# Attention in two levels of Strassen products: the sums of K's second chunk ten slots later, and the first batch's V sums later in the opening

## The chip, the cores and the metric

The kernel runs on one core of one Trainium2 chip. The metric is the time of one execution on the device, in microseconds, as the median of several runs. A core has a matrix engine (TensorE, PE in the profile), a vector engine (VectorE, DVE), a scalar engine (ScalarE, ACT), GpSimd (POOL) and SyncE (SP). Each runs its own list of instructions in the order in which the program wrote them; semaphores tie the lists together. Here SyncE issues the stores of the output and the DMA transposes, and GpSimd issues the loads.

## What is computed

For 8 batches, q, k and v are 2048 x 512 (float32, normal random numbers):

```python
scores = np.matmul(q, k.transpose(0, 2, 1)) / np.sqrt(d_k)
attn_weights = special.softmax(scores, axis=-1).astype(np.float32)
return np.matmul(attn_weights, v)
```

## The kernel before

**Products.** All matrices are cast to float16, and sums of products are float32 in PSUM. Both matrix products are done in a form of Strassen's method: a product of 2 x 2 blocks is made with seven block products instead of eight, and pays for it with sums of blocks ahead of them and sums of results behind them. For Q K^T the operands' sums are four per chunk of K (`k_sums`, lines 181 to 190; the four are L185, L186, L187 and L188, in that order, and L186 overwrites a block of K in place) and four per 1024 queries of Q (`q_sums`, L202 to L205). For P V they are four per half of V (`v_sums`, L219 to L222) and four per tile of P (`p_sums`, L368 to L371). Some P V products are split a second time (`fine`, lines 500 to 550; its sums are `a_sums`, L494 to L497, and `vi_sums`, L241 to L244). The operands' sums are all on VectorE.

**Results.** `Group` (line 285) makes the scores of 256 keys by 1024 queries with its seven products (L317). Product 5 starts a PSUM bank z, product 3 adds to it, and VectorE's L342 (`after3`) adds z to a tile `cz` and so empties the bank; L339 (`after7`) does the same for the bank x after product 7. ScalarE copies and takes the exponential (L253; the one over `cz` is the largest). `Pair` (line 378) multiplies P by V (L414), and its results are scaled by the reciprocal of the row sums, which a column of ones in V gives (L423 on ScalarE, L426 on VectorE). In `fine`, ScalarE's L530 and L534 copy partial results out of PSUM, and VectorE's L536 and L541 add them.

**Order.** The order is written out by hand. The work goes in 32 periods, four per batch (`qt` = 0 to 3), each of 28 slots. A slot holds one product of a Group, for the scores of the next 1024 queries, and often one product of a Pair for the output of the present period. Beside each slot stand the sums that VectorE is to do there (`sums_of`, line 615) and the loads, transposes and K sums for the next batch (`prefetch`, line 601). A slot thus sets a place in each engine's list and not a time.

**The next batch's K.** K comes in four chunks of 512 keys. For each, GpSimd loads it with a cast into a staging tile (two of these exist), SyncE transposes it by DMA into the tile `kraw` of that chunk (L150), and VectorE then does the four sums. `PLAN` (line 577) gives the slots of loads and transposes; for the second chunk the transpose stands at slot 8 of period 1 and for the third at slot 20 of period 1. `KSUMS` (line 592) gives the slots of the sums, counted through the batch's four periods: 39 is slot 11 of period 1, 56 is slot 0 of period 2. All this is done in the first seven batches, for the batch that follows. The first Group of the next batch that uses the second chunk begins at slot 14 of period 2; its product with the first sum stands at slot 16, with the third at slot 17, and with the fourth at slot 19.

**The opening.** Ahead of the periods stand 14 slots with the first scores of the first batch, in which VectorE takes one sum per slot from a list called `background` (line 599; `step`, line 758). In the first period `SUMS0` (line 661) names VectorE's sums: "v11" is the sum number 1 of the half 1 of V. The half 0 of V is loaded by two transfers and the half 1 by the two last ones of the opening.

Of the kernel before, what the change touches and what calls it, by code (L numbers as in the profile page):

```python
# [12 lines left out]
def kernel(  # L13
# [153 lines left out]
    def pe_transpose(what, c, n0=0, n1=CH):  # L167
        for n in range(n0, n1, 2):
            transposed(what, c, n, 2, nc.scalar.copy if n and n0 != n else nc.vector.tensor_copy)
# [28 lines left out]
    def q_sums(sp):  # L198
        b11, b12, b21, b22 = q_blocks(sp)
        t1, t2, t4 = qsum  # L200
        return [
            lambda: sub(t1[:], b12, b11),  # L202
            lambda: sub(t2[:], b22, t1[:]),
            lambda: sub(t3_of(sp), b22, b12),
            lambda: sub(t4[:], b21, t2[:]),  # L205
        ]
# [6 lines left out]
    def v_sums(b, c):  # L213
        vh = vraw[b % 2]
        js = slice(c * NI, (c + 1) * NI)
        b11, b12 = vh[:, js, 0, 0:H], vh[:, js, 0, H:D]
        b21, b22 = vh[:, js, 1, 0:H], vh[:, js, 1, H:D]
        return [
            lambda: sub(vt1[:, js, 0:H], b12, b11),  # L219
            lambda: sub(vt2[:, js], b22, vt1[:, js, 0:H]),  # L220
            lambda: sub(b12, b22, b12),
            lambda: sub(vt4[:, js], b21, vt2[:, js]),  # L222
        ]
# [31 lines left out]
    def plain_tile(kb, half, name):  # L255

        st = bank(name)
        c, n = divmod(kb, CH)
        for dc in range(ND):
            nc.tensor.matmul(  # L260
                st[:], kops[c][0][:, n, dc, :], qraw[0][:, half * NT:(half + 1) * NT, dc, :],
                start=(dc == 0), stop=(dc == ND - 1),
            )
        left, right = pts[0]
        exp(right[:, kb // 2, kb % 2, :] if half else left[kb % 2][:, kb // 2, :], st[:])
# [89 lines left out]
    def p_sums(g, which, j0=0, j1=NJ):  # L355

        left, right = pts[g // 2]
        if (g, which) not in psums:
            psums[g, which] = [
                spool.tile([P, NJ, P], F16, tag=f"s{n}", name=f"s{n}") for n in (1, 2, 4)  # L360
            ]
        s1, s2, s4 = psums[g, which]
        cols = columns(g, which)
        js = slice(j0, j1)
        a11, a21 = left[0][:, js, cols], right[:, js, 0, cols]
        a12, a22 = left[1][:, js, cols], right[:, js, 1, cols]
        return [
            lambda: add(s1[:, js], a21, a22),  # L368
            lambda: sub(s2[:, js], s1[:, js], a11),  # L369
            lambda: sub(a21, a11, a21),  # L370
            lambda: sub(s4[:, js], a12, s2[:, js]),  # L371
        ]
# [205 lines left out]
    for qt_, slot_, *what_ in (  # L578
# [13 lines left out]
    KSUMS = {  # L592
        divmod(slot, NS): (c, n)
        for c, slots in (
            (0, (39, 42, 43, 44)), (1, (46, 48, 56, 59)), (2, (67, 71, 74, 76)), (3, (84, 86, 88, 90))
        )
        for n, slot in enumerate(slots)
    }
    background = deque()
# [15 lines left out]
    def sums_of(g, slot):  # L615
# [43 lines left out]


    SUMS0 = {
# [96 lines left out]
    def step(n=1):  # L758
        for _ in range(min(n, len(background))):
            background.popleft()()  # L760
# [19 lines left out]
    for slot in range(14):  # L780
        n, at = divmod(slot, len(QORDER))
        old, what = QORDER[at]
        if slot == 3:
            background.extend(p_sums(0, "a", 0, NG))
            background.append(v_sums(0, 0)[0])
        if slot == 7:
            background.extend((v_sums(0, 1)[0], v_sums(0, 0)[1]))
        if at == 0:
            cur = Group(0, 6 + n)
        if old == 0:  # L790
            cur.product(what)
        elif prev is not None:
            prev.product(what)
        if at == 2 and prev is not None:
            prev.exp_right()
        if at == len(QORDER) - 1:
            prev = cur
        if slot in TILES:
            plain_tile(*tiles.pop(0), "px")
        if slot in (8, 10):  # L800
            pe_transpose("q", 3, slot - 8, slot - 6)
        if slot in (10, 12, 13):
            q_sums(1)[max(slot - 11, 0)]()
        step()
# [56 lines left out]
```

## Time and profile before

| | |
|---|---|
| median of 3 runs | 823.46 us (822.53 to 823.62) |
| the profiled execution | 824.57 us |
| its span, first to last instruction | 822.5 us |
| mean granted TensorE clock in it | 0.996 |
| VectorE busy | 677.8 us |
| ScalarE busy | 609.1 us |
| HBM traffic over the span | 163 GB/s |

The profile is one execution. A row of a table of instructions gives the source line, the engine, the operation, the tile written, an arrow and the tiles read, the shapes, how many there were, their busy time and what ended the idle time before them. A row of a timeline begins with the start and the length in microseconds, and ends, in brackets, with how long the engine had been idle before and which engine, tile and line released it. SPq and POOLq are issues of DMAs. TensorE's ends are modelled, so its busy time is not a measure of its efficiency; its idle time, which is what the waits show, is read from starts.

### The profile page before, as it was taken

What the parts mean: (1) busy time and instruction counts of PE and PEld (TensorE: products, weight loads), DVE (VectorE), ACT (ScalarE), POOL (GpSimd) and SP (SyncE); (2) the same over time, 40 slices, a digit from 0 to 9 for tenths busy, and PEclk for the clock granted to TensorE, in tenths of its full rate; (3) what the DMA queues carried; (4) which work ended last, traced back from release to release, by engine and by line L of the source; (5) the groups of instructions that cost most, each with busy time, mean ns of one, the idle gap of its engine ahead of it and who ended that gap; (6) DMA issues with size and microseconds to landing.
All of it is one profiled execution on the core that took longest, in us unless ns stands there. A gap on an engine that the chain in (4) does not pass through costs nothing.

```text
span 822.5 us, 16565 instructions
## 1 busy us (share of the span) xinstructions
PE 792.6 (96%) x6226; PEld 537.8 (65%) x6226; DVE 677.8 (82%) x1568; ACT 609.1 (74%) x1194; POOL 72.1 (9%) x106
## 2 busy tenths in 40 slices
PE   8999899998999899997999989999899998999998
PEld 5556566665666566665666656666566665666676
DVE  3788788969899698995889968898788987889774
ACT  4678677876877777776777877878687776787752
POOL 4011110101100110001100011001110101000000
PEclk9999999999999999999999999999999999999999
DMA  9989992899928999289983899657994679811112
GB/s 220 167 145 141 170 215 70 160 155 194 172 60 162 159 185 173 70 155 140 188 168 78 154 154 196 138 109 147 162 198 103 139 140 173 164 55 53 52 52 103
DMA packets 188160, 115.96 MB, mean 141 GB/s; under 512 B 122288, under 2 KB 170800, under 8 KB 188080
## 3 DMA queue, kind: packets, MB, share of 16 engines
q0 software_dynamic: 49648, 49.29, 41.0%
q1 hardware_dynamic: 138144, 65.29, 34.5%
q8 instruction: 48, 0.79, 0.4%
q10 hardware_dynamic: 288, 0.33, 0.1%
q14 instruction: 32, 0.26, 0.1%
HBM read 100.73 MB, written 33.55 MB: 163 GB/s over the span
## 4 chain that ended last, share of the span: by engine, by line
PE 79%; DMA 16%; DVE 3%; ACT 1%; issue 1%; POOL 0%; DVEq 0%; ACTq 0%
PE t L317 38%; PE t L414 31%; DMA kraw<-stage 12%; PE t L519 10%; DMA vh<-in_v_dram 3%; DMA right<-in_q_dram 1%; ACT right L253 1%; DVE cz L342 1%; DMA first<-in_k_dram 1%; DVE cz L339 0%; DVE o L426 0%; DVE s L369 0%; DVE left L496 0%; DVE kraw L186 0%; POOL stage L124 0%
## 5 line engine op out<-in xcount | busy, mean ns | idle before, releaser
L317 PE MATMUL t<-qraw,kraw 128*128 128x512 f16 x728 | 206.4, 379 | 0.2 <-ACT left L253 0.2
L414 PEld LDWEIGHTS <-s 128*128 128x128 f16 x1536 | 150.5, 98 | 60.0 <-issue 1.6
L253 ACT ACTIVATE left<-t 128x512 f16<-128x512 f32 (+1 forms) x260 | 155.7, 602 | 23.3 <-PE t L317 17.4
L423 ACT ACTIVATE o<-t,r 128x256 f32<-128x256 f32 x256 | 116.1, 483 | 56.1 <-DVE r L443 30.1
L317 PE MATMUL t<-qs,ks 128*128 128x512 f16 x488 | 136.1, 381 | 19.2 <-DVE cz L342 19.2
L253 ACT ACTIVATE right<-cz 128x1024 f16<-128x1024 f32 x122 | 129.3, 1060 | 17.0 <-DVE cz L339 16.3
L414 PE MATMUL t<-vt,s 128*128 128x257 f16 (+1 forms) x1024 | 135.6, 275 | 0.0
L414 PEld LDWEIGHTS <-right 128*128 128x128 f16 x1024 | 100.2, 98 | 37.2 <-issue 0.5
L333 ACT COPY cz<-t 128x512 f32<-128x512 f32 x120 | 70.3, 586 | 68.2 <-PE t L317 65.3
L317 PEld LDWEIGHTS <-kraw 128*128 128x128 f16 x976 | 90.5, 98 | 44.9 <-issue 1.0
L426 DVE SCALAR_TENSOR_TENSOR o<-t,r,o 128x256 f32<-128x256 f32 x192 | 92.2, 480 | 23.2 <-ACT o L530 8.9
L317 PEld LDWEIGHTS <-ks 128*128 128x128 f16 x732 | 66.6, 97 | 59.7 <-issue 21.3
L339 DVE TENSOR_TENSOR cz<-t,cz 128x512 f32<-128x512 f32 x122 | 83.7, 686 | 22.2 <-PE t L317 21.5
L519 PEld LDWEIGHTS <-left 128*128 128x128 f16 x928 | 69.2, 98 | 45.4 <-issue 5.2
L342 DVE TENSOR_TENSOR cz<-t,cz 128x512 f32<-128x512 f32 x122 | 83.8, 687 | 13.7 <-PE t L317 7.1
L328 ACT COPY t<-t 128x512 f32<-128x512 f32 x120 | 69.0, 575 | 20.0 <-PE t L317 15.9
L317 PE MATMUL t<-qs,kraw 128*128 128x512 f16 x244 | 73.2, 382 | 0.1
L317 PE MATMUL t<-qraw,ks 128*128 128x512 f16 x244 | 72.5, 378 | 0.0
L336 ACT COPY cz<-t 128x512 f32<-128x512 f32 x122 | 71.1, 583 | 0.0
L519 PE MATMUL t<-vh,left 128*128 128x128 f16 x696 | 67.6, 219 | 3.0 <-ACT o L530 3.0
L414 PE MATMUL t<-vh,s 128*128 128x257 f16 x512 | 66.9, 272 | 0.2 <-ACT o L423 0.2
L414 PE MATMUL t<-vt,right 128*128 128x256 f16 x512 | 66.2, 273 | 0.3 <-DVE o L426 0.3
(85 smaller groups left out, 937.2 us busy)
## 6 DMA issues: line engine op xcount, KB each, us to landing
out_dram<-o SPq DMA_DIRECT2D x127, 256.0 KB, 2.9
vh<-in_v_dram POOLq DMA_DIRECT2D x32, 512.0 KB, 10.2
stage<-in_q_dram POOLq DMA_DIRECT2D x28, 512.0 KB, 6.7
stage<-in_k_dram POOLq DMA_DIRECT2D x28, 512.0 KB, 6.4
right<-in_q_dram POOLq DMA_DIRECT2D x2, 512.0 KB, 9.9
right<-in_k_dram POOLq DMA_DIRECT2D x2, 512.0 KB, 12.1
first<-in_q_dram SPq DMA_DIRECT2D x2, 256.0 KB, 3.9
cz<-in_q_dram SPq DMA_DIRECT2D x2, 256.0 KB, 4.9
```

Of the source, the lines that this page charges most:

```text
L253: nc.scalar.activation(out=out_, in_=in_, func=EXP, scale=inv_sqrt_d)
L317: nc.tensor.matmul(dst[:], lhs[:, j, dc, :], rhs[:, :, dc, :], start=(n in (1, 5) and dc == 0), stop=(dc == 1), skip_group_check=True,)
L328: f(out=self.y[:], in_=self.x[:])
L333: f(out=self.cz[:, 1, :], in_=self.z[:])
L336: nc.scalar.copy(out=self.cz[:, 0, :], in_=self.x[:])
L339: nc.vector.tensor_add(self.cz[:, 1, :], self.x[:], self.cz[:, 1, :])
L342: nc.vector.tensor_add(self.cz[:, 0, :], self.z[:], self.cz[:, 0, :])
L414: nc.tensor.matmul(dst[:, 0:width], lhs(j), rhs(j), start=(first and j == 0), stop=(j == NJ - 1), skip_group_check=True,)
L423: nc.scalar.activation(out=out_, in_=src, func=COPY, scale=r[:])
L426: nc.vector.scalar_tensor_tensor(out=out_, in0=src, scalar=r[:], in1=out_, op0=MULT, op1=ADD)
L519: nc.tensor.matmul(dst, lhs[:, j, :], rhs[:, j, :], start=(n == 1 and j == 0), stop=(j == NI - 1), skip_group_check=True,)
```

## The change

```diff
@@ -592,7 +592,7 @@
     KSUMS = {
         divmod(slot, NS): (c, n)
         for c, slots in (
-            (0, (39, 42, 43, 44)), (1, (46, 48, 56, 59)), (2, (67, 71, 74, 76)), (3, (84, 86, 88, 90))
+            (0, (39, 42, 43, 44)), (1, (56, 59, 60, 65)), (2, (67, 71, 74, 76)), (3, (84, 86, 88, 90))
         )
         for n, slot in enumerate(slots)
     }
@@ -659,7 +659,7 @@
     SUMS0 = {
-        2: "v11", 4: "q3", 5: "a0", 6: "a1", 8: "a3", 9: "a2", 
+        2: "v01", 3: "v11", 4: "q3", 5: "a0", 6: "a1", 8: "a3", 9: "a2", 
         12: "v20", 14: "b0 v21", 15: "v30", 16: "b1",
@@ -782,9 +782,8 @@
         if slot == 3:
             background.extend(p_sums(0, "a", 0, NG))
-            background.append(v_sums(0, 0)[0])
         if slot == 7:
-            background.extend((v_sums(0, 1)[0], v_sums(0, 0)[1]))
+            background.extend(v_sums(0, 0)[0:2])
         if at == 0:
             cur = Group(0, 6 + n)
```

The four sums of the second chunk move from slots 18 and 20 of period 1 and 0 and 3 of period 2 to slots 0, 3, 4 and 9 of period 2. In VectorE's list the first sum now stands where the third stood, behind two instructions of period 1's last Pair; the second, third and fourth follow three to ten instructions apart.

In the opening, the first sum of V's half 0 keeps its place in VectorE's list, because four sums of P are ahead of it in `background` either way. The first sum of V's half 1, which came next, moves to slot 2 of the first period, and the second sum of the half 0 takes the place that it leaves. The second sum of the half 1 moves from slot 2 to slot 3, right behind.

The numbers of instructions on every engine are the same before and after, and the lists of TensorE, ScalarE, GpSimd and SyncE hold the same instructions in the same order.

## The prediction

> **What bounds the kernel now.** I read the page first, then the table of waits, then the timelines of the places that the waits name. The page's first part and its chain by engine:
>
> ```profile
> PE 792.6 (96%) x6226; PEld 537.8 (65%) x6226; DVE 677.8 (82%) x1568; ACT 609.1 (74%) x1194; POOL 72.1 (9%) x106
> ...
> PE 79%; DMA 16%; DVE 3%; ACT 1%; issue 1%; POOL 0%; DVEq 0%; ACTq 0%
> ```
>
> TensorE is busy 792.6 of 822.5 us, so about 30 us of it can be idle at most, and yet 16% of the chain is DMA. Something makes the end wait for transfers now and then. The table of waits, of TensorE and then of VectorE (total us, times, longest):
>
> ```profile
> PE t L317 <- DVE cz L342: 19.2, 7, 4.2
> PE t L519 <- ACT o L530: 3.0, 5, 0.6
> PE t L728 <- DVE warm L683: 1.2, 1, 1.2
> PE t L260 <- DVE qraw L163: 1.0, 1, 1.0
> ```
>
> ```profile
> DVE ks L185 <- DMA kraw<-stage: 31.5, 7, 6.0
> ```
>
> TensorE waits seven times, 19.2 us in all, for VectorE's add of line 342; VectorE waits seven times, 31.5 us, in the first sum of a K chunk (L185) for the DMA transpose that writes this chunk. Seven is the number of batches for which a next batch is prepared. The timelines of the second of the seven, VectorE, then TensorE, then ScalarE:
>
> ```profile
> 181.62 0.17 DVE L477 RECIPROCAL r<-t 128x1 f32<-128x1 f32 x1 [0.48 <-PE t L414]
> 185.70 0.42 DVE L185 TENSOR_TENSOR ks<-kraw 128x512 f16<-128x512 f16 x1 [3.90 <-DMA kraw<-stage]
> 186.04 0.68 DVE L342 TENSOR_TENSOR cz<-t,cz 128x512 f32<-128x512 f32 x1
> ...
> 188.17 0.68 DVE L339 TENSOR_TENSOR cz<-t,cz 128x512 f32<-128x512 f32 x1
> ...
> 193.68 0.41 DVE L187 TENSOR_TENSOR ks<-ks,kraw 128x512 f16<-128x512 f16 x1
> ```
>
> ```profile
> 186.78 0.59 PE L317 MATMUL t<-qs,ks 128*128 128x512 f16 x2 [2.14 <-DVE cz L342]
> ...
> 190.15 0.39 PE L519 MATMUL t<-vh,left 128*128 128x128 f16 x4 [0.59 <-ACT o L530]
> ```
>
> ```profile
> 188.88 1.06 ACT L253 ACTIVATE right<-cz 128x1024 f16<-128x1024 f32 x1 [0.89 <-DVE cz L339]
> 189.85 0.25 ACT L530 COPY o<-t 128x128 f32<-128x128 f32 x1
> ```
>
> This is one event from end to end. At 181.8 VectorE reaches the first sum of K's second chunk and stands 3.90 us. Behind it in VectorE's order stands L342, which empties the PSUM bank that the next fifth product needs: TensorE stands 2.14 us. L339 is late too, so ScalarE's exponential is late, L530 behind it is late, and TensorE stands 0.59 us more. Of VectorE's wait the first 3.90 - 2.14 = 1.76 us cost nothing. The row at 193.68, the third sum, marks slot 0 of the next period (39 of the sums' list is slot 11 of period 1, so 56 is slot 0 of period 2): there the change puts the first sum.
>
> **The change, part 1: K's second chunk.** Per batch four VectorE instructions of 0.42 us move from slots 18 and 20 of period 1 and slots 0 and 3 of period 2 to slots 0, 3, 4 and 9 of period 2. No instruction is added and no DMA moves. In the order written for VectorE, L342, L426, L339 and the rest of period 1 come ahead of the wait.
>
> The first batch's wait shows the same (TensorE):
>
> ```profile
> 87.57 0.59 PE L317 MATMUL t<-qs,ks 128*128 128x512 f16 x2 [3.07 <-DVE cz L342]
> ```
>
> Term a: the seven waits for L342, 19.2 us, go. Term b: the five waits for L530, 3.0 us, go, because their cause is the same late L339.
>
> Term c: the granted clock. The third batch's wait and the fourth's (TensorE):
>
> ```profile
> 286.54 0.59 PE L317 MATMUL t<-qs,ks 128*128 128x512 f16 x2 [2.71 <-DVE cz L342]
> ```
>
> ```profile
> 388.69 0.59 PE L317 MATMUL t<-qs,ks 128*128 128x512 f16 x2 [4.18 <-DVE cz L342]
> ```
>
> The stretches right behind these two, by the busy time by stretch (the column before the last two is the granted clock):
>
> ```profile
> 287.26:290.67 3.41, 3.41 (x18) 2.10 (x16) 3.41 (x8) 2.19 (x4) 1.48 (x2) 0.50 1.01 142
> 389.66:393.07 3.41, 3.41 (x16) 1.80 (x14) 3.38 (x8) 1.94 (x4) 1.48 (x2) 0.50 1.12 155
> ```
>
> After each, the clock is halved for 3.41 us, in which TensorE shows busy and does half the work: 2 x 1.7 = 3.4 us more. The L530 wait is missing in just these two batches, so b and c do not overlap.
>
> [...] By the rows the term is 3.4, and I take that.
>
> What is late next? (i) The wait itself, ten slots on. The latest case is the fourth batch, whose wait is VectorE's longest. From the chain, then VectorE's timeline:
>
> ```profile
> 372.57 15.02 DMA kraw<-stage
> ```
>
> ```profile
> 387.62 0.42 DVE L185 TENSOR_TENSOR ks<-kraw 128x512 f16<-128x512 f16 x1 [5.95 <-DMA kraw<-stage]
> ...
> 396.36 0.41 DVE L187 TENSOR_TENSOR ks<-ks,kraw 128x512 f16<-128x512 f16 x1
> ```
>
> The transfer lands at 372.57 + 15.02 = 387.59. Slot 0 came at 396.36; without TensorE's 4.18 and the 1.7 of the clock it comes at 390.5, so 2.9 us are left. In the second batch it is 193.68 - 2.14 - 0.59 - 185.70 = 5.3 us. The transfer starts, and nearly ends, before the stall begins, so it gains nothing and loses nothing when the stall goes. I cost the new place at 0; if this cover were used up, VectorE could still wait about 1.8 us (above) before TensorE notices.
>
> (ii) VectorE's load. The stretch from slot 18 of a period to slot 13 of the next, once across a batch's border (no K sums of the second chunk in it, but V's) and once at the changed place; columns are length, TensorE, weight loads, VectorE:
>
> ```profile
> 132.80:152.80 20.00, 20.00 (x160) 13.65 (x159) 18.97 (x44) 15.37 (x32) 0.74 (x1) 1.00 0.47 104
> 181.40:204.10 22.70, 19.96 (x157) 13.31 (x156) 18.23 (x43) 15.46 (x31) 2.22 (x3) 1.00 1.08 193
> ```
>
> The same TensorE work, 20.0 us, runs without a gap in the first with 18.97 us of VectorE beside it. The changed place has 18.23, before and after the move, so VectorE can keep pace; slot by slot the border carries V's sums of 0.6 us in slots 0 and 3 and V's inner sums in 7 and 11, more than the four K sums add. I value this at 0. The bounds: below 0 only by what VectorE's fewer sums in slots 18 and 20 could hasten, where no other wait stands, so nothing; above, each of the four 0.42 us on TensorE's path in all seven batches, 11.8 us. I take the lower end, since the nearest row, the border, shows no wait.
>
> (iii) The third chunk. Its transpose in the first batch (SyncE), slot 0 there, and its first sum (VectorE):
>
> ```profile
> 86.70 3.05 SPq L150 DMA_TRANSPOSE kraw<-stage  x1
> ```
>
> ```profile
> 94.48 0.42 DVE L187 TENSOR_TENSOR ks<-ks,kraw 128x512 f16<-128x512 f16 x1
> ...
> 103.05 0.42 DVE L185 TENSOR_TENSOR ks<-kraw 128x512 f16<-128x512 f16 x1
> ```
>
> Issued at 86.70, with the median time to landing of all transposes (the row quoted next) it is there at about 91; its sum moves up by under 6 us, to 97 or later. Nothing is late there.
>
> ```profile
> DMA to landing us min/median/max: 4.3/4.6/18.8
> ```
>
> **Part 2: the first batch's V.** VectorE and TensorE in the opening:
>
> ```profile
> 37.33 0.68 DVE L333 COPY cz<-t 128x512 f32<-128x512 f32 x1
> 39.96 0.69 DVE L219 TENSOR_TENSOR vt<-vh 128x1024 f16<-128x1024 f16 x1 [1.95 <-DMA vh<-in_v_dram]
> 40.57 0.68 DVE L163 COPY qraw<-tr 128x1024 f16<-128x1024 f16 x1
> 41.29 0.69 DVE L202 TENSOR_TENSOR qs<-qraw 128x1024 f16<-128x1024 f16 x1
> ```
>
> ```profile
> 41.31 1.02 PE L260 MATMUL t<-qraw,kraw 128*128 128x512 f16 x4 [1.04 <-DVE qraw L163]
> ```
>
> The L219 at 39.96 is the first sum of V's second half; it waits for the last V load, and L163 behind it, which empties a PSUM bank, holds TensorE 1.04 us. In the new order the second sum of V's first half stands there; its data is long in place, so L163 starts at about 37.9 + 0.6 = 38.5 and TensorE goes on at 40.3. The moved sum follows L339, some 2 us after the load landed, and stands directly ahead of the next sum of the same half, whose place in the order does not change. Term d: 1.0 us. Its bounds are 0 (another wait takes the place) and 1.04.
>
> **The sum.** 19.2 + 3.0 + 3.4 + 1.0 = 26.6 us of the profiled execution's 824.57 us (2.1 of it outside the span of 822.5). That execution lies 1.1 us above the median of 823.46; the same 26.6 off the median gives 823.46 - 26.6 = 796.9. A check by the period: slot 0 of the first batch is at 94.48, that of the seventh at 694.74 (row below), 600.3 us for six batches. The second to the seventh lose 19.2 - 3.1, four L530 waits of 0.6 and the 3.4, together 21.9 of it, which leaves 96.4 us a batch. From the fourth's slot 0 (396.36) to the seventh's are 298.4 us, 99.5 a batch with only a and b in them. The two agree with some 3 us a batch to gain.
>
> ```profile
> 694.74 0.41 DVE L187 TENSOR_TENSOR ks<-ks,kraw 128x512 f16<-128x512 f16 x1
> ```
>
> **The rivals.**
> R1, the wait goes along: VectorE stands at slot 0 of period 2 instead. For it: the same transfer took 12.95 us in the second batch and 15.02 in the fourth (its rows), so it varies by 2 us, and only 2.9 are left at the tightest. Against: 5.3 in the other. If it came out 7 us later in every batch, VectorE would stand 2 to 4 us and, with 1.8 us covered, TensorE 0 to 2, some 1 us: 797 + 7 = 804.
> R2, VectorE crowded: the four sums in one stretch push the adds behind them. Half of the bound of 11.8 us gives 803. For it: VectorE is busy 18.2 of the 20 us; against: the border's row, with more.
> R3, slower than before: the same transfer, but landing so late that the stop in period 2 is longer than today's. The gain is 26.6 / 7 = 3.8 us a batch, so TensorE must lose more than 3.8 there; with 5.3 + 1.8 us of cover that is a landing over 10.9 us later, a transfer of some 24 us instead of 13. At 26 it is 5.9 us of loss a batch: 797 + 41 = 838. Only a transfer that collides with more than its present neighbours would do that, and no transfer is moved against it before it lands.
> R4, part 2 does not do what it says: L163's bank is free earlier, but TensorE stops at the next thing, for instance at L202, which waits for a Q transpose that lands only about 39.3 (row below, and the longest landing, 18.8). Then term d is 0: 797.9.
>
> ```profile
> 20.51 7.22 SPq L150 DMA_TRANSPOSE qraw<-right  x1
> ```
>
> R5, the half clock has causes of its own: one of the two halvings stays, 798.6. [...] The other five waits, of up to 3.1 us, had none behind them, so waits of this size are at the edge.
>
> **How the numbers follow.** Forecast, all four terms: 0.70. R1 0.07, R2 0.08, R3 0.03, R4 0.07, R5 0.03; no difference at all 0.01, and 0.01 for a slower one of another kind. The likeliest gives 796.9. Small stops that cannot be seen in the table can make it 2 us less, 795; upward the range takes in R4, R5 and the greater part of R1 and R2, 803. A run of this kernel can tell about 0.2%, 1.6 us, from no change. Faster 0.95, within 0.2% 0.01, slower 0.04.
>
> **What would show it.** Right: in the table of waits of the changed kernel L317 <- L342 and L519 <- L530 are gone, L185 <- DMA is under 2 us in all, no stretch with a clock of 0.50, and L260 <- L163 is gone; slot 0 of one batch follows that of the last after about 96.4 us. R1 shows as L185 <- DMA of several us at slot 0; R2 as short TensorE waits for L342, L339 or L496 in period 2 with VectorE busy throughout; R4 as another wait at 40 us. Wrong in the whole: a batch of 99 us as before.

## The result, and the profile after

| | before | changed |
|---|---|---|
| median of 4 runs each | 823.0 us (819.02 to 823.62) | 796.1 us (794.98 to 797.54) |
| ratio, 95% interval | | 0.9684 (0.9649 to 0.9719) |
| profiled execution, its span | 824.57, 822.5 us | 795.86, 793.8 us |

The change gains 26.9 us by the medians, where 26.6 were forecast. The page of the changed kernel, engines and chain:

```profile
PE 787.4 (99%) x6226; PEld 537.0 (68%) x6226; DVE 678.0 (85%) x1568; ACT 608.4 (77%) x1194; POOL 72.3 (9%) x106
...
PE 96%; DMA 2%; ACT 1%; DVE 1%; issue 0%; ACTq 0%
```

TensorE's busy time is smaller by 5.2 us although its instructions are the same. About 3.4 of it is the work of the two stretches of half clock (3.41 us each at a granted clock of 0.50), now done at full speed; the rest comes from the ends of the records beside the waits, which are explained below. The chain is TensorE almost alone. The first rows of TensorE's table of waits, and VectorE's two waits for a DMA (total, times, longest):

```profile
PE t L728 <- DVE warm L683: 1.2, 1, 1.2
PE t L519 <- DVE si L497: 0.5, 1, 0.5
PE t L260 <- DVE kraw L163: 0.3, 1, 0.3
PE t L414 <- DVE o L426: 0.3, 1, 0.3
```

```profile
DVE ks L185 <- DMA kraw<-stage: 1.0, 1, 1.0
DVE qs L202 <- DMA qraw<-right: 0.8, 1, 0.8
```

L317 behind L342, L519 behind L530 and the opening's 1.0 us behind L163 are gone. Of VectorE's 31.5 us for K's chunks 1.0 is left, and that is for the third chunk, in the first batch; it brings the one new wait of TensorE, 0.5 us behind L497. The same place as in the second batch before, in VectorE's timeline of the changed kernel:

```profile
176.34 0.17 DVE L477 RECIPROCAL r<-t 128x1 f32<-128x1 f32 x1 [0.47 <-PE t L414]
176.84 0.69 DVE L342 TENSOR_TENSOR cz<-t,cz 128x512 f32<-128x512 f32 x1 [0.33 <-PE t L317]
...
185.18 0.41 DVE L185 TENSOR_TENSOR ks<-kraw 128x512 f16<-128x512 f16 x1
```

L342 now starts as soon as TensorE has released it, half a microsecond behind L477 and not 4.4 us. The sum L185 stands at slot 0 without a bracket, so nothing was waited for. The transfer was no quicker; in the table of DMA issues, which gives the time to landing, that of the changed kernel's second batch, issued at 167.44:

```profile
kraw<-stage SPq DMA_TRANSPOSE x1, 14.0
```

It landed at 181.4, 3.7 us ahead of slot 0 (5.3 forecast). In the fourth batch it was 4.1 us ahead (2.9 forecast), and over the seven batches 3.7 to 4.7. The seventh batch's slot 0:

```profile
665.89 0.41 DVE L185 TENSOR_TENSOR ks<-kraw 128x512 f16<-128x512 f16 x1
```

From the second batch to the seventh that is 480.7 us, 96.1 a batch, and from the first to the seventh 96.3 (96.4 forecast).

**Where the 28.7 us between the two spans came from.** I compared the start of each matmul with that of the same matmul in the other trace; the difference grows in steps. The step at the second batch's wait, before (first fence) and changed (second):

```profile
184.04 0.59 PE L317 MATMUL t<-qraw,kraw 128*128 128x512 f16 x2
```

```profile
178.75 0.59 PE L317 MATMUL t<-qraw,kraw 128*128 128x512 f16 x2
179.18 0.59 PE L317 MATMUL t<-qs,ks 128*128 128x512 f16 x2
```

Before, the next start was 186.78, 2.74 us on; now it is 0.43 us on. The step is 2.31 us where the table of waits said 2.14. A row of two matmuls is 0.59 us long and one is 0.38 (page, mean 379 ns), so the second starts 0.21 after the first; a wait is counted from the end of a record, and 0.16 us of that record would have lain beside the next one. Each wait therefore cost about 0.16 us more than its row says. Summed so: seven L342 waits 20.3 us (19.2 by the rows), five L530 waits 3.8 (3.0), two half clocks 3.2 (3.4), the opening 1.6 (1.0) with 0.4 more from a first load that landed earlier (TensorE's first L137 starts at 3.89 us and not at 4.29), and -0.7 for the new wait. Together 28.6 of 28.7. The medians, 26.9 apart, are of several executions each, and the kernel before varies more than this one: 819.02 to 823.62 against 794.98 to 797.54, with a mean granted clock of 0.990 to 0.998 in its executions beside the experiments, where the changed kernel's has 0.999 and 1.0.

### The profile page after: what moved, and what is told of

It reads as the page before. It is cut to its first block, busy times and chain, and to the rows that moved or that the text cites. A ratio compares the mean times of both kernels' runs of the same rounds, so it can differ in the third digit from the quotient of the medians.

```text
span 793.8 us, 16565 instructions
## 1 busy us (share of the span) xinstructions
PE 787.4 (99%) x6226; PEld 537.0 (68%) x6226; DVE 678.0 (85%) x1568; ACT 608.4 (77%) x1194; POOL 72.3 (9%) x106
## 4 chain that ended last, share of the span: by engine, by line
PE 96%; DMA 2%; ACT 1%; DVE 1%; issue 0%; ACTq 0%
PE t L317 45%; PE t L414 36%; PE t L519 11%; PE t L260 2%; DMA kraw<-stage 2%; PE tr L160 1%; PE tr L137 0%; PE t L728 0%; PE t L276 0%; ACT left L253 0%; DVE o L426 0%; ACT o L423 0%; ACT right L253 0%; DVE kraw L163 0%; DVE cz L342 0%
## 5 line engine op out<-in xcount | busy, mean ns | idle before, releaser
L317 PE MATMUL t<-qraw,kraw 128*128 128x512 f16 x728 | 206.4, 379 | 0.1
L253 ACT ACTIVATE left<-t 128x512 f16<-128x512 f32 (+1 forms) x260 | 156.1, 603 | 22.3 <-PE t L317 16.7
L423 ACT ACTIVATE o<-t,r 128x256 f32<-128x256 f32 x256 | 116.4, 486 | 59.7 <-DVE r L443 32.9
L253 ACT ACTIVATE right<-cz 128x1024 f16<-128x1024 f32 x122 | 129.5, 1061 | 10.0 <-DVE cz L339 9.7
L317 PE MATMUL t<-qs,ks 128*128 128x512 f16 x488 | 135.2, 379 | 0.0
L414 PE MATMUL t<-vt,s 128*128 128x257 f16 (+1 forms) x1024 | 133.8, 273 | 0.0
L317 PEld LDWEIGHTS <-kraw 128*128 128x128 f16 x976 | 90.3, 98 | 44.3 <-issue 0.6
L426 DVE SCALAR_TENSOR_TENSOR o<-t,r,o 128x256 f32<-128x256 f32 x192 | 92.2, 481 | 27.0 <-PE t L414 11.9
L339 DVE TENSOR_TENSOR cz<-t,cz 128x512 f32<-128x512 f32 x122 | 83.7, 686 | 22.2 <-PE t L317 21.6
L519 PEld LDWEIGHTS <-left 128*128 128x128 f16 x928 | 68.9, 98 | 41.1
L342 DVE TENSOR_TENSOR cz<-t,cz 128x512 f32<-128x512 f32 x122 | 83.8, 687 | 14.6 <-PE t L317 8.3
L317 PEld LDWEIGHTS <-ks 128*128 128x128 f16 x732 | 66.5, 97 | 39.4 <-issue 0.2
L328 ACT COPY t<-t 128x512 f32<-128x512 f32 x120 | 69.0, 575 | 19.2 <-PE t L317 14.9
L317 PE MATMUL t<-qs,kraw 128*128 128x512 f16 x244 | 72.5, 379 | 0.0
L317 PE MATMUL t<-qraw,ks 128*128 128x512 f16 x244 | 72.5, 378 | 0.0
L519 PE MATMUL t<-vh,left 128*128 128x128 f16 x696 | 67.4, 219 | 0.0
## 6 DMA issues: line engine op xcount, KB each, us to landing
right<-in_q_dram POOLq DMA_DIRECT2D x2, 512.0 KB, 10.2
```

What stands on the lines that cost most here:

```text
L253: nc.scalar.activation(out=out_, in_=in_, func=EXP, scale=inv_sqrt_d)
L317: nc.tensor.matmul(dst[:], lhs[:, j, dc, :], rhs[:, :, dc, :], start=(n in (1, 5) and dc == 0), stop=(dc == 1), skip_group_check=True,)
L328: f(out=self.y[:], in_=self.x[:])
L339: nc.vector.tensor_add(self.cz[:, 1, :], self.x[:], self.cz[:, 1, :])
L342: nc.vector.tensor_add(self.cz[:, 0, :], self.z[:], self.cz[:, 0, :])
L414: nc.tensor.matmul(dst[:, 0:width], lhs(j), rhs(j), start=(first and j == 0), stop=(j == NJ - 1), skip_group_check=True,)
```

## The experiments

**The two parts alone.** For `e1_k_alone` the changed `KSUMS` stands in the kernel before:

```diff
-(1, (46, 48, 56, 59))
+(1, (56, 59, 60, 65))
```

> The sums of K's second chunk alone, the opening as before. Theory (the seven waits of TensorE, the L530 waits behind them and the two half clocks all come from the K sums' place; the V sums are a term of their own): the time lies 25 to 27 us under before, 796 to 798, and 1 to 2 us over the changed kernel; L260 <- L163 of about 1.0 us stays, L317 <- L342 is gone. Rival (the two parts work together, the opening's gain makes room for the rest): less than 23 us of the gain is left.

Measured: 797.43 us (797.32 to 797.7), ratio 0.9697 (0.9671 to 0.9723) to a before of 821.93. TensorE's waits:

```profile
PE t L260 <- DVE qraw L163: 1.3, 1, 1.3
PE t L728 <- DVE warm L683: 1.2, 1, 1.2
```

The time is the theory's 796 to 798; the gain of 24.5 us is just under its 25 to 27, as this before is at 821.93, and well over the rival's 23. No wait behind L342 is left, and the opening's wait stays by itself. `e2_v_alone` is the changed kernel with the old `KSUMS` row:

```diff
-(1, (56, 59, 60, 65))
+(1, (46, 48, 56, 59))
```

> The V sums of the opening alone, K's sums at their old slots. Theory: 1 to 2 us faster than before, 821 to 822; seven waits L317 <- L342 of 19 us in all stay, with half a clock behind some of them. Rival (no other kind of gain): within 0.5 us of before.

Measured: 821.89 us (821.0 to 823.4), ratio 0.9986 (0.9969 to 1.0004). By time this decides nothing, since it meets the theory's 821 to 822 and lies within 0.5 us of the before beside it, 821.93 (820.01 to 826.63); the theory's gain of 1 to 2 us does not show. The trace shows the opening's wait gone, but also another draw of the large waits: six behind L342, 16.5 us in all, with three half clocks. In the first batch there is none, because the second chunk's transfer took only 5.3 us there. The opening's share is read better between `e1_k_alone` and the changed kernel, where no large wait blurs it: 1.3 us by the medians (from two sets of runs), and 1.8 by the starts of the same matmuls.

**Does it matter what stands behind the wait?** `e3_one_slot` puts K's first sum one slot later than before, just behind L342:

```diff
-(1, (56, 59, 60, 65))
+(1, (47, 49, 56, 59))
```

> The changed kernel with K's first two sums at slots 19 and 21 of period 1 instead of 18 and 20, and the other two at their old slots: the first sum stands one place further, just behind the L342 that TensorE waited for. Theory (what matters is which instruction stands behind the wait): VectorE still waits about 3 us in each of seven batches, L317 <- L342 and the half clocks are gone, and at most waits of about 0.6 us for L530 or the like stay: 797 to 801. Rival (what matters is how long VectorE stands, whatever is behind it, less the 1.76 us that before covered): TensorE waits some 1.2 us a batch for something else, and with the L530 waits the time is 805 to 811.

Measured: 815.98 us (813.71 to 820.21), ratio 0.9935 (0.9901 to 0.997). The theory fell, and the rival is nearer though too low. TensorE's waits, then those of VectorE:

```profile
PE t L317 <- DVE cz L339: 11.3, 6, 2.2
PE t L519 <- ACT o L530: 3.9, 6, 0.7
```

```profile
DVE ks L185 <- DMA kraw<-stage: 21.3, 7, 3.6
```

L342 is gone from the table and the next add, L339, has taken its place. In the code it holds TensorE as hard: product 4 adds into the bank x that L339 reads after product 7. The second batch, VectorE and TensorE:

```profile
181.07 0.42 DVE L185 TENSOR_TENSOR ks<-kraw 128x512 f16<-128x512 f16 x1 [2.89 <-DMA kraw<-stage]
...
182.94 0.68 DVE L339 TENSOR_TENSOR cz<-t,cz 128x512 f32<-128x512 f32 x1
```

```profile
183.67 0.59 PE L317 MATMUL t<-qs,kraw 128*128 128x512 f16 x2 [1.50 <-DVE cz L339]
```

VectorE stands 2.89, TensorE 1.50: 1.39 us are covered here, against 1.76 behind L342. So what TensorE loses at its first wait is VectorE's stand less a cover of 1.4 to 1.8 us, with L342 as with L339 as the add that holds it. A place with neither of them behind it was not tried here. There are six such waits because in the first batch, as in `e2_v_alone`, the second chunk's transfer took 5.3 us; VectorE's seventh wait is for the first chunk. The two kinds of waits with their 0.16 us each make 17.1 us on the changed kernel's span, 810.9, and this span is 811.6. That profiled execution is the fastest of the five, 813.71. The others were not profiled; their mean granted clocks, 0.992 to 0.998 against 1.0, point to half clocks in them.

**Late enough, and no more.** `e5_four_slots` has the first sum four slots later than before, behind this L339 too:

```diff
-(1, (56, 59, 60, 65))
+(1, (50, 53, 56, 59))
```

> The changed kernel with K's first sum at slot 22 of period 1 (four slots later than before instead of ten), the second at 25, the third and the fourth at slots 0 and 3 of period 2. Theory (TensorE feels VectorE's stand less the 1.4 to 1.8 us that VectorE is ahead, whatever instruction is behind it): VectorE still stands 1 to 2.2 us in six or seven batches, 8 to 13 us in all, and TensorE waits under 3 us in all: 796 to 799, within 0.4% of the changed kernel. Rival (what counts is that no add of cz stands behind the wait; every stand goes through): TensorE waits 1 to 2 us a batch, 804 to 811.

Measured: 796.5 us (795.91 to 797.86), ratio 0.9685 (0.9653 to 0.9718). VectorE's waits:

```profile
DVE ks L185 <- DMA kraw<-stage: 0.4, 2, 0.2
DVE qs L202 <- DMA qraw<-right: 0.4, 1, 0.4
```

The time is the theory's, but VectorE stood for 0.4 us only. The instructions ahead of the sum, two of which (L342 and L426) wait for TensorE, bring VectorE there about when the transfer lands: in the second batch the transfer landed at 180.54 and the sum began at 180.56. The run therefore does not test the cover; it shows that four slots are enough here and that the other six bring nothing that can be measured.

**Why the transfer is late.** `e4_v_load_later` leaves all sums of the kernel before where they were and moves one load:

```diff
-(1, 12, "load", "v", 1)
+(1, 24, "load", "v", 1)
```

> The kernel before, with the second V load of the next batch at slot 24 of period 1 instead of slot 12; the sums stay where they were. Theory (the transfer of K's second chunk takes 13 to 15 us because it shares the DMA engines with two loads): it takes 8 to 11 us, lands 3 to 5 us earlier, VectorE's waits fall from 31.5 to under 12 us in all, TensorE's for L342 from 19.2 to under 4, and the time is 798 to 806. Rival (the transfer is slow by itself, or through the other load alone): it still takes 12.5 us or more, and the time is 817 or more.

Measured: 802.44 us (801.34 to 804.4), ratio 0.976 (0.9734 to 0.9786). The transfer of the second batch (issues of the table of DMAs, this kernel), VectorE's wait and TensorE's:

```profile
kraw<-stage SPq DMA_TRANSPOSE x1, 11.1
```

```profile
DVE ks L185 <- DMA kraw<-stage: 11.7, 7, 2.1
```

```profile
PE t L519 <- ACT o L530: 3.5, 7, 0.6
PE t L728 <- DVE warm L683: 1.2, 1, 1.2
PE t L260 <- DVE qraw L163: 1.1, 1, 1.1
PE t L317 <- DVE cz L342: 0.6, 2, 0.3
```

As the theory said: one load less beside it, and the transfer takes 11.1 us and not 12.95; VectorE stands at most 2.1 us, and L317 behind L342 falls from 19.2 to 0.6 us with every sum at its old slot. The waits behind L530 stay, 3.5 us in seven batches against 3.0 in five. The third batch, VectorE and TensorE:

```profile
277.21 0.43 DVE L185 TENSOR_TENSOR ks<-kraw 128x512 f16<-128x512 f16 x1 [1.56 <-DMA kraw<-stage]
```

```profile
281.66 0.39 PE L519 MATMUL t<-vh,left 128*128 128x128 f16 x4 [0.56 <-ACT o L530]
```

This stand is shorter than the lead of 1.76 us over L342, and still costs TensorE 0.56 us by way of L339, ScalarE's exponential and L530: over that second path the lead is only 1.0 us, the same in the four batches here in which L342 held nobody. Both waits together, with 0.16 us for each row, come to the stand less about 0.85 us in all seven batches here (1.56 gives 0.72) and in the five of the kernel before that had no half clock (3.90 gives 2.31 + 0.75); in `e3_one_slot` they come to the stand less about 0.4 (2.89 gives 1.66 + 0.81).

The cause of the old time is thus shown from both ends: a transfer stretched by its neighbours, and a sum that stood too near its landing. `e7_both_v_load` does the same to the changed kernel, with the same diff:

> The changed kernel with the second V load of the next batch at slot 24 of period 1 instead of 12. Theory (both remove the same wait): no further gain beyond 0.7 us, 795 to 797.5; VectorE does not wait for K's second chunk, the transfer takes 10 to 11 us. Rival (the collision of transfers costs something besides this wait): 792 or less.

Measured: 795.33 us (795.18 to 796.8), ratio 0.9673 (0.9641 to 0.9704), against 796.32 of the changed kernel on the same chip. VectorE waits for no K chunk at all, and from the second batch on the transfer takes 10.2 to 11.1 us, as expected. The intervals overlap, so a further gain is not shown.

**How full is the new place?** `e6_doubled` does three of the four sums twice, with the same results:

```diff
             k_sums(c)[n]()
+            if c == 1 and n != 1:
+                k_sums(c)[n]()
```

> The changed kernel with the first, third and fourth sum of K's second chunk done twice at their new slots (1.0 us more of VectorE a batch between slots 0 and 9 of period 2; the results are the same). Theory (VectorE has 1 to 2 us to spare there, as the stretch across the batch's border shows): TensorE's waits grow by under 2 us in all, 796 to 799. Rival (the new place is full already): up to 1 us a batch shows, 801 to 804.

Measured: 803.01 us (802.63 to 803.42), ratio 0.9761 (0.9724 to 0.9799). The rival was right: 6.7 us over the 796.32 beside it, about 1 us a batch. The new wait (0.67 us by its row and 0.16 more by the starts, each batch), in TensorE's table of this kernel, then ScalarE around it in the second batch of the changed kernel, and of this one:

```profile
PE t L317 <- ACT left L253: 4.7, 7, 0.7
```

```profile
194.14 0.47 ACT L423 ACTIVATE o<-t,r 128x256 f32<-128x256 f32 x1 [0.33 <-DVE r L443]
194.51 0.59 ACT L253 ACTIVATE left<-t 128x512 f16<-128x512 f32 x1
```

```profile
196.64 0.47 ACT L423 ACTIVATE o<-t,r 128x256 f32<-128x256 f32 x1 [1.27 <-DVE r L443]
197.01 0.59 ACT L253 ACTIVATE left<-t 128x512 f16<-128x512 f32 x1
```

VectorE's reciprocal L443 stands behind the fourth sum. ScalarE waits for it in L423, the exponential L253 stands behind L423, and L253 empties the bank that TensorE's next product needs. In the changed kernel that product starts without a wait; here it is the row below.

```profile
197.65 0.59 PE L317 MATMUL t<-qraw,kraw 128*128 128x512 f16 x2 [0.67 <-ACT left L253]
```

A sum and its repeat took 0.87 us where one took 0.41, so 1.4 us were added a batch, and 1.0 came through: about 0.4 us of room is left at the new place. Of the 1.0 us, 0.83 are this wait; the other 0.15 come a little earlier, at an L519 that waits for VectorE's sum L494, too short a stop for the table of waits.

**Once more.** `e8_again` is the changed kernel itself.

> The changed kernel once more, on the chip of the three runs beside it. Theory: 795 to 798; whether the first batch's VectorE wait of 1.0 us for K's third chunk and TensorE's 0.5 us behind it come again shows if they belong to the program or to that execution: I expect them again, within 0.5 us, since more transfers are in flight there than before. Rival (chance): no such wait.

Measured: 796.32 us (795.04 to 796.84), ratio 0.9678 (0.9646 to 0.971). My expectation on the first batch missed: the third chunk's wait did not come again. VectorE's one wait for a K chunk is now at another place:

```profile
74.46 0.43 DVE L185 TENSOR_TENSOR ks<-kraw 128x512 f16<-128x512 f16 x1 [1.29 <-DMA kraw<-stage]
```

This is the first chunk, and TensorE lost 0.3 us behind L497 by it. `e2_v_alone` and `e3_one_slot` wait at this chunk too, 1.7 and 1.6 us. Which transfer of the first batch is late differs from execution to execution; why was not settled.

## Why the prediction was right, point by point

- **The mechanism** (VectorE held at a DMA wait, adds behind it, TensorE behind those) was right. `e1_k_alone` gives 24.5 us by moving the sums, `e4_v_load_later` 19.5 by hastening the transfer.
- **Terms a and b**, 19.2 and 3.0: both gone, worth 20.3 and 3.8. The rows were read rightly; what was missed is the 0.16 us that a wait hides.
- **Term c**, 3.4: gone, worth 3.2. The two stretches of half clock are in no part of the changed kernel's work (R5 fell).
- **Term d**, 1.0: worth 1.6 in the trace, 1.3 by the medians of `e1_k_alone` and the changed kernel. R4's stop at L202 came, 0.8 us on VectorE, and held nobody. The bound of 1.04 was too low, since two small waits right behind it went as well.
- **Step (i)**, the new place costs 0: right; 3.7 us were left in the second batch. R1 and R3 did not come. The reserve of 1.8 us behind it, read from L342 alone, was not needed; at the old place it was too large, since in `e4_v_load_later` TensorE lost time by L530 from a stand of about 1.0 us on.
- **Step (ii)**, VectorE keeps pace: right for this load, and the reason was too weak. The border's busy time of 18.97 of 20 us said nothing of the one reciprocal with 0.4 us of room; with 1.4 us more a batch VectorE is crowded as R2 has it, though the wait came behind ScalarE's L253 and not behind the adds that R2 named.
- **Step (iii)**, "Nothing is late there": wrong in this execution. The third chunk's transpose in the first batch took 13.9 us, VectorE stood 1.0 us and TensorE 0.5. I had taken the median of all transposes, 4.6 us, for one that runs beside loads and stores; in the profile before, this one had taken 7.5.
- The sum of 26.6 us is right to 0.3 by the medians; between the two profiled executions it is 28.7, and the missing 2.1 are the hidden 0.16 us a wait, the opening and the earlier first load, less the new wait of 0.7. So the close agreement of the medians is partly luck: the terms were read in one execution with two half clocks, and executions of the kernel before differ by 4 us and more.

## What to carry to other kernels

VectorE's wait, in its ordered list, cost what stood behind it; price such a wait as the stand less the lead that the engine has (here 1.76 us over L342, 1.39 over L339 and 1.0 over L530), over each path by which another engine waits for it and not over the first alone, and do not hope that the next instruction is harmless: behind L339 TensorE still waited 11.3 us. Look for the landing of the transfer, put its first reader behind an instruction that is naturally that late, and ask as well which neighbours stretch the transfer: moving one load gave 19.5 us, where the whole change gave 26.9. Before filling a place with work, find the one instruction there with the least room (0.4 us at L443 here), since a stretch's busy share did not show it.

## What the runs showed of the hardware

**Waits of 2.6 to 3.1 us had half a clock behind them or had none.** The three stretches of half clock in `e2_v_alone` (0.50, the column before the last two), and two at full speed between them:

```profile
182.94:186.35 3.41, 3.41 (x19) 2.21 (x18) 3.41 (x9) 2.19 (x4) 1.16 (x2) 0.50 0.83 122
281.93:285.34 3.41, 1.74 (x16) 1.22 (x16) 2.82 (x7) 0.58 (x1) 1.24 (x2) 1.00 0.86 154
285.34:288.75 3.41, 2.82 (x26) 1.78 (x24) 3.37 (x9) 2.62 (x6) 0.98 (x2) 1.00 1.21 159
384.33:387.74 3.41, 3.41 (x20) 2.32 (x19) 3.41 (x8) 2.28 (x4) 1.48 (x2) 0.50 0.94 126
684.70:688.11 3.41, 3.41 (x16) 1.96 (x14) 3.32 (x7) 1.94 (x5) 1.48 (x2) 0.50 1.12 155
```

TensorE's waits in this run include these:

```profile
182.63 0.75 PE L317 MATMUL t<-qs,ks 128*128 128x512 f16 x2 [2.81 <-DVE cz L342]
...
283.60 0.59 PE L317 MATMUL t<-qs,ks 128*128 128x512 f16 x2 [3.00 <-DVE cz L342]
...
584.05 0.59 PE L317 MATMUL t<-qs,ks 128*128 128x512 f16 x2 [2.82 <-DVE cz L342]
...
683.68 0.59 PE L317 MATMUL t<-qs,ks 128*128 128x512 f16 x2 [2.57 <-DVE cz L342]
```

The wait of 3.00 us had no half clock behind it (the second and the third row above, full speed), the shorter one of 2.57 had; 2.81 had one and 2.82 had none. Before, a half clock followed 2.71 us, and none followed 3.07. So the length of a wait did not decide it alone, and what else does was not shown. Where a half clock came, the wait cost 1.6 us more (3.2 for the two before). In `e3_one_slot` the waits of L317 go up to 2.23 us, and its profile has no half clock between the opening and the end (mean granted clock 1.0).

**The DMA transposes of 512 rows took 4.3 us at the least, and three times as long beside two loads.** That of K's second chunk took 12.8 to 15.0 us beside two loads in before's profile, and 11.1 us in the second batch of `e4_v_load_later`, where one of the two is moved; the least, 4.3 us, is in the prediction's row of times to landing.
